# Reordering the first mixer's projections, the first loads and the last block's transposes in a two-layer trunk

## The chip, the cores and the metric

The kernel runs on one core of one Trainium2 chip. The core has five engines with a queue each: PE (TensorE, matrix products into PSUM, and PE transposes), DVE (VectorE), ACT (ScalarE), POOL (GpSimd) and SP (SyncE, which here only issues transfers). Each engine executes its queue in order. The metric is the device time of one execution in microseconds, as the median of several runs.

## The reference

A trunk of two layers works on x of 256 positions by 2048 features, all in float32. Each layer is a mixer and a squared-ReLU MLP of width 8192, each with an RMS norm ahead of it and a residual sum behind it. The mixer of the first layer has two halves that share one projection `h @ w_in`:

```
aq, ak, av, bqkv, bz, ba, bb = split(h @ w_in)
oa = diff_attention(rope(norm(aq)), rope(norm(ak)), av, lam)   # 8 heads of 128, 2 sub-heads each
bq, bk, bv = split(silu(conv4(bqkv)))
ob = gated_delta_rule(l2(bq), l2(bk), bv, g(ba), sigmoid(bb))  # 8 heads, a linear recurrence
ob = rms(ob) * silu(bz)
x = x + concat(rms(oa), ob) @ w_out
x = x + squared_relu_mlp(norm(x))
```

The second layer has a dilated attention for its mixer and the same kind of MLP.

## The kernel before

**Products.** Every large product goes through `dense` (L191). It takes 512 weight columns and the 16 chunks of 128 features that they are summed over. For each chunk ACT rounds the weights to a short float (L204, the tile `..h`) and DVE forms the remainder (L205 through the helper L107, the tile `..l`); for each of the two halves of 128 positions PE then runs three products (L210, L211, L212: high by high, high by low, low by high). So a chunk is six products of 128x128 by 128x512, and a `dense` of 16 chunks is 96 of them. Weights arrive in tiles of two chunks, loaded by `wload` (L171) on SP's queue. Four PSUM tiles (`psd`, L101) let two products be under way at once: the next one needs two tiles that the one before the last has given back.

**The activations.** `xt_block` (L261) turns 512 columns of x into four chunks: PE transposes into PSUM, ACT writes the short float with the norm's gain, DVE the remainder. PSUM for transposes has two tiles (`pst`, L102).

**What runs between the chunks.** Smaller work is written as Python generators in three streams: "g" holds the recurrences g0 to g3 (`gdn`, L600, two heads each), "s" the convolutions (`qk_conv`, `v_side`) and the attention pairs d0 to d3 (`diff`, L854), "o" the output norms. After every chunk `drip` (L182) emits the next step of one stream: "g" and "s" in turn, "o" with every fourth chunk. A stream works through its generators one behind the other. `flush` (L165) emits steps of all streams with no chunk between them, until a condition holds. A scheduler then fixes the order on each engine: earliest emitted first among what its own model of time calls ready, so a later product can be put ahead of a step whose operands are not there.

**The order of the first mixer** is written out by hand (L976 to L997): `b0 z2 bv0 b1 z0 av0 a0 b2 bv1 b3 z1 a1 av1 a2 a3`. Here `b` is queries and keys of two recurrent heads (they start a convolution and then a recurrence g), `bv` values of four recurrent heads, `z` the output gate, `a` queries and keys of an attention pair (they start d), `av` values of four attention heads. A recurrence g starts when the one before has ended and its own convolved queries and keys are there. Its steps: normalise keys (`kh`), transpose them (`kt`), products `pk` and the matrix `m`, which is written to DRAM (`scm`) and read back as small diagonal blocks (`mb`), transpose `tt1`, inversion of the blocks on DVE (`tm`, `ta`, `xc`), which goes to DRAM (`scx`) and comes back as two full matrices (`xy`, 512 KB), products `pa` with `am` and transpose `tt2`, four empty steps, two levels `lp`, `ly`, `lx`, then `lpz`, `lyz`, `pu`, `ps`, `pv`, `po`. `gdn_out` norms the result, multiplies it by the gate `sz` and transposes it (`ot`).

**The mixer's end.** Behind `a3` all recurrences are flushed, x is loaded again into `xs0` to `xs3`, and the output projection runs in two parts of eight chunks: `wo00` to `wo03` use heads 0 to 3 of each kind, then, behind another flush, `wo10` to `wo13` use the rest. The tiles `xs0`, `xs1` take the memory of the values of recurrent heads 0 to 3 and 4 to 7; `xs2`, `xs3` take that of the gate `sz`. So `xs1` can be loaded when `pu` of g3 has read its values and `xs2`, `xs3` when g3's output has been multiplied by the gate; each product is added to its `xs` tile (`add_to_x`) before its PSUM is given back.

**The beginning** (L350 to L394): eight products of a tile of zeros with itself (`pw`, L358), then the loads: the left half of the first x block (256 columns), on ACT's queue the identity and the norm's gains, then on SP the first weights of `b0`, and only then the right half of the first x block (L371). Behind the first block's transposes stand four more products into `pw` (L394), whose result nobody reads.

**Between the parts.** `next_norm` (L295) is the generator that sums the squares of a block of x (ACT) and transposes it for the next part; the last block, n = 3, does it while the next part's first product runs.

Of the kernel before, what the change touches and what calls it, by code (L numbers as in the profile page):

```python
# [19 lines left out]
P = 128  # L20
# [67 lines left out]
def trunk(  # L88
# [4 lines left out]
    nc = tc.nc  # L93
    V, S, G, E = nc.vector, nc.scalar, nc.gpsimd, nc.tensor
# [17 lines left out]
    def stt(o, a, s, b, op0, op1):  # L112
        V.scalar_tensor_tensor(out=o, in0=a, scalar=s, in1=b, op0=op0, op1=op1)
# [7 lines left out]
    def act(o, a, f, scale=1.0, bias=0.0, accum=None):  # L121
        if accum is None:
            S.activation(out=o, in_=a, func=f, scale=scale, bias=bias)  # L123
        else:
            S.activation(out=o, in_=a, func=f, scale=scale, bias=bias, accum_out=accum)
# [4 lines left out]
    def ps_t(name):  # L130
        return pst.tile([P, 512], F32, tag="t", name=name)

    def ps_m(name):
        return psm.tile([P, 512], F32, tag="m", name=name)

    def quads(t, n=4):
        return t.rearrange("p (c d) -> p c d", c=n)
# [30 lines left out]
                step(q)  # L168


    def wload(wsrc, k0, nm):  # L171
        raw = wp.tile([P, 2, 512], F32, tag="wr", name=f"{nm}r{k0}")
        off = 0
        for s in wsrc:
            m = s.shape[1]
            nc.sync.dma_start(raw[:, :, off:off + m], s[k0 * P:(k0 + 2) * P, :].rearrange("(c p) n -> p c n", p=P))
            off += m
        return raw

# [11 lines left out]
    def dense(wsrc, stat, kcs, nm, pre=(), every=1, unit=1):  # L191

        n = sum(s.shape[1] for s in wsrc)
        ps = [psd.tile([P, 512], F32, tag="d", name=f"{nm}p{h}") for h in range(NH)]
        first, last = kcs[0], kcs[-1]
        for j, kc in enumerate(kcs):
            if j % 2 == 0:
                raw = pre[j // 2] if j // 2 < len(pre) else wload(wsrc, kc, nm)
            if j % unit == 0:
                w = raw[:, j % 2:j % 2 + unit, :n]  # L200
                whs = wq[0].tile([P, unit, 512], F32R, tag="wh", name=f"{nm}h{kc}", bufs=6 // unit)[:, :, :n]
                wls = wq[0].tile([P, unit, 512], F32R, tag="wl", name=f"{nm}l{kc}", bufs=6 // unit)[:, :, :n]
                with tc.high_priority(offset=AHEAD):
                    cast[0] = S.copy(whs, w)  # L204
                    tt(wls, w, whs.bitcast(F32), ALU.subtract)  # L205
            wh, wl = whs[:, j % unit], wls[:, j % unit]
            for h in range(NH):
                sh, sl = stat(kc, h)
                o = ps[h][:, :n]
                E.matmul(o, lhsT=sh, rhs=wh, start=kc == first, stop=False)  # L210
                E.matmul(o, lhsT=sh, rhs=wl, start=False, stop=False)  # L211
                E.matmul(o, lhsT=sl, rhs=wh, start=False, stop=kc == last)  # L212
            if j % every == 0:
                drip()
        return ps
# [12 lines left out]
    def cst(name):  # L228
        lo, hi = COLS[name]
        return ca[:, lo:hi]  # L230

    ident = cst("ident")

    def transpose(o, i, k=P):
        E.transpose(o, i, ident[:k, :k])
# [12 lines left out]
    def x_tile(n, nm):  # L248
        return cp.tile([P, NH, 512], F32, tag=f"x{n}", name=f"{nm}{n}")

    def stats_block(xt, n, nm):
        for h in range(NH):
            j = sp.tile([P, 512], F32, tag="junk", name=f"{nm}j{h}")
            act(j, xt[:, h, :], AF.Square, accum=ssqp[:, h, n:n + 1])

    def stats_end(nm):
        s = sp.tile([P, NH], F32, tag="ssq2", name=nm + "s")
        rsum(s, ssqp)
        rsqrt(rstd, s, NH, 1.0 / D, nm)

    def xt_block(xt, n, norm, nm, dst, pool=None):  # L261

        if pool is not None:
            xT = pool.tile([P, 4, T], F32, tag="hT", name=nm + "T", bufs=2)
            for i in range(4):
                turn_quadrant(xt, xT, i)
                yield
        xh = xp.tile([P, 4, T], F32R, tag="xh", name=nm + "h")
        xl = xp.tile([P, 4, T], F32R, tag="xl", name=nm + "l")
        dst.append((xh, xl))  # L270
        for c2 in range(2):
            if pool is None:
                t = quads(ps_t(f"{nm}t{c2}"), 2)
                for c in range(2):
                    for h in range(NH):
                        k = c2 * 2 + c
                        transpose(t[:, c, h * P:(h + 1) * P], xt[:, h, k * P:(k + 1) * P])
            else:
                t = xT[:, 2 * c2:2 * c2 + 2, :]
            for c in range(2):  # L280
                k = c2 * 2 + c
                g = gt[:, norm * 16 + n * 4 + k:norm * 16 + n * 4 + k + 1]
                act(xh[:, k, :], t[:, c, :], AF.Identity, scale=g)
                stt(xl[:, k, :], t[:, c, :], g, xh[:, k, :].bitcast(F32), ALU.mult, ALU.subtract)
            yield

    def turn_quadrant(src, dst, i):

        q = slice(32 * i, 32 * i + 32)
        sv = src[q].rearrange("p h (c j f) -> p h c j f", c=4, j=4)  # L290
        for j in range(4):
            dv = dst[32 * j:32 * j + 32].rearrange("p c (h t) -> p h c t", h=NH)
            V.transpose(out=dv[:, :, :, q], in_=sv[:, :, :, j, :])  # L293

    def next_norm(n, norm, nm, dst, pool=None):  # L295

        stats_block(xs[n], n, nm + "s")
        yield from xt_block(xs[n], n, norm, nm, dst, pool if n < 3 else None)
        if n == 3:
            stats_end(nm + "e")  # L300
            yield
# [41 lines left out]
    xv = x[0].rearrange("(h p) d -> p h d", p=P)  # L343
# [3 lines left out]
    def b_cols(s):  # L347
        return [win[:, 3072 + s * 256:3328 + s * 256], win[:, 4096 + s * 256:4352 + s * 256]]
# [6 lines left out]
    pw = ps_m("pw")  # L355
# [3 lines left out]
    xq = [x_tile(n, "xq") for n in range(4)]  # L359
    pre = []  # L360
    for n in range(4):
        if n == 0:
            nc.sync.dma_start(xq[0][:, :, :256], xv[:, :, :256])
            nc.scalar.dma_start(ca[:, :P], consts[:, :P])
            nc.scalar.dma_start(grow0, ab_norm[0].rearrange("(c p) -> c p", p=P))
        else:
            nc.sync.dma_start(xq[n], xv[:, :, n * 512:(n + 1) * 512])
        if n < 3:
            pre.append(wload(b_cols(0), 2 * n, "b0"))
        if n == 0:  # L370
            nc.sync.dma_start(xq[0][:, :, 256:], xv[:, :, 256:512])  # L371
    with ExitStack() as mix:
        wq[0] = mix.enter_context(tc.tile_pool(name="wq0", bufs=1))
        op = mix.enter_context(tc.tile_pool(name="op", bufs=1))
# [13 lines left out]
        for n in range(4):  # L388
            for _ in xt_block(xq[n], n, 0, f"xa{n}", xb):
                pass  # L390
            if n == 0:

                for _ in range(4):
                    E.matmul(pw[:, :P], lhsT=ident, rhs=xq[0][:, 1, 256:384], start=True, stop=True)  # L394


        cga = cp.tile([P, NH, 2, 64], F32, name="cga")
# [538 lines left out]
        def do_b(s, pre=()):  # L936
            ps = dense(b_cols(s), xstat, KC16, f"b{s}", pre)
            flush(lambda: "rstd" in ready)
            streams["s"].append(qk_conv(raw_evac(ps, f"b{s}raw"), f"b{s}raw", s, qks))
            streams["g"].append(gdn_of(s))  # L940
# [6 lines left out]
        def do_bv(g):  # L947
            ps = dense([win[:, 5120 + g * 512:5632 + g * 512]], xstat, KC16, f"bv{g}")
            rv = raw_evac(ps, f"bv{g}raw")
            vbs[g] = cp.tile([P, NH, 4, P], F32, tag=f"x{g}", name=f"vb{g}")  # L950
            streams["s"].append(v_side(rv, f"bv{g}raw", g, vbs[g], f"bv{g}"))

        def do_a(s):
            ps = dense([win[:, s * 256:(s + 1) * 256], win[:, 1024 + s * 256:1280 + s * 256]], xstat, KC16, f"a{s}")
            r = raw_evac(ps, f"a{s}raw")
            streams["s"].append(diff_of(r, s))
# [6 lines left out]
        def do_av(g):  # L963
            ps = dense([win[:, 2048 + g * 512:2560 + g * 512]], xstat, KC16, f"av{g}")
            va = mp.tile([P, NH, 512], F32, tag="va", name=f"va{g}", bufs=2)
            for h in range(NH):
                act(va[:, h, :], ps[h], AF.Identity, scale=rstd[:, h:h + 1])
            vas[g] = va
# [11 lines left out]
        bz_evac(ps, 776, 248, "z2")  # L980
        streams["s"].append(gates(ga, gb))
        do_bv(0)
        do_b(1)
        ps = dense([win[:, 6144:6656]], xstat, KC16, "z0")
        bz_evac(ps, 0, 512, "z0")
        ready.add("z0")
        do_av(0)
        do_a(0)
        do_b(2)
        do_bv(1)  # L990
        do_b(3)
        ps = dense([win[:, 6656:6920]], xstat, KC16, "z1", every=2)
        bz_evac(ps, 512, 264, "z1")
        ready.add("z1")
        do_a(1)
        do_av(1)
        do_a(2)  # L997
        do_a(3)
# [185 lines left out]
```

## Time and profile before

| what | us |
|---|---|
| median of 3 runs | 2296.64 (2295.28 to 2297.88) |
| the profiled execution's own time | 2296.41 |
| its span, first instruction to last | 2294.6 |
| PE busy in the span | 2281.6 |

The first mixer fills the span up to about 514 us. `L210 PE MATMUL wo13p` means that PE ran a product of line 210 into the PSUM tile of the product `wo13`; digits that are only buffer numbers are left out of names, so `xs` stands for all four blocks. A product of the steady stream is shown with about 0.39 us, but they overlap: one starts every 0.23 us. Times are counted from the span's start.

### The profile page before, as it was taken

To read this page: it belongs to the slowest core of one execution; us is meant where nothing else is said; L and a number is where in the kernel's file an instruction comes from. 1 tells how busy PE (TensorE), PEld (TensorE's weight loads), DVE (VectorE), ACT (ScalarE), POOL (GpSimd) and SP (SyncE) were. 2 spreads that over 40 slices of the span, in tenths; PEclk is the share of its full clock that TensorE was granted. 3 is DMA by queue.
4 is the path that set the end of the run, shared out by engine and by line. 5 is a ranking of instruction groups with operands and counts; after the bars stand their busy time and mean duration, and the time that the engine had idled before them with its cause. 6 is when DMAs were issued, how large, how long until landed. Compare 5 with 4: busy or idle time off the path is not lost.

```text
span 2294.6 us, 29903 instructions
## 1 busy us (share of the span) xinstructions
PE 2281.6 (99%) x10544; PEld 1890.9 (82%) x10544; DVE 1666.3 (73%) x3027; ACT 1195.8 (52%) x1865; POOL 5.7 (0%) x15
## 2 busy tenths in 40 slices
PE   9999999999999999999999999999999999999999
PEld 8887878788888888888888888888888888888887
DVE  6868787867747846846888888986775775775774
ACT  7657656655534534534545555555543543543553
POOL 0000000000000000000000000000000000000000
PEclk9999999999999999999999999999999999999999
DMA  8655455456666666666666555555666666666665
GB/s 257 185 171 167 138 176 144 140 174 195 200 193 190 196 194 189 196 197 190 192 190 199 177 180 176 174 184 165 193 193 195 193 194 195 192 196 193 188 208 165
DMA packets 271482, 426.54 MB, mean 186 GB/s; under 512 B 22322, under 2 KB 102372, under 8 KB 271332
## 3 DMA queue, kind: packets, MB, share of 16 engines
q1 hardware_dynamic: 271156, 424.56, 61.1%
q8 instruction: 82, 1.34, 0.2%
q14 instruction: 68, 0.56, 0.1%
q10 hardware_dynamic: 176, 0.07, 0.0%
HBM read 420.11 MB, written 4.46 MB: 185 GB/s over the span
## 4 chain that ended last, share of the span: by engine, by line
PE 95%; DVE 3%; DMA 1%; ACT 1%; issue 0%; SPq 0%; ACTq 0%
PE m_0p L211 3%; PE n_2p L211 3%; PE n_1p L212 3%; PE n_0p L212 3%; PE m_3p L212 3%; PE m_3p L210 3%; PE m_2p L212 3%; PE m_2p L210 3%; PE m_1p L212 3%; PE m_1p L210 3%; PE n_1p L211 3%; PE n_0p L210 3%; PE n_2p L212 3%; PE m_0p L212 3%; PE n_2p L210 3%; PE n_0p L211 3%
## 5 line engine op out<-in xcount | busy, mean ns | idle before, releaser
L107 DVE TENSOR_TENSOR n_3l<-n_3r,n_3h 128x1024 fp32r<-128x1024 f32 x64 | 78.4, 1224 | 76.8 <-ACT n_3h L204 76.7
L107 DVE TENSOR_TENSOR n_2l<-n_2r,n_2h 128x1024 fp32r<-128x1024 f32 x64 | 78.4, 1224 | 76.8 <-ACT n_2h L204 76.7
L107 DVE TENSOR_TENSOR m_0l<-m_0r,m_0h 128x1024 fp32r<-128x1024 f32 x64 | 78.1, 1225 | 73.4 <-ACT m_0h L204 73.0
L107 DVE TENSOR_TENSOR n_1l<-n_1r,n_1h 128x1024 fp32r<-128x1024 f32 x64 | 78.4, 1224 | 67.8 <-ACT n_1h L204 67.2
L204 ACT CAST n_2h<-n_2r 128x1024 fp32r<-128x1024 f32 x64 | 67.5, 1054 | 100.2 <-PE n_2p L212 59.9
L204 ACT CAST n_3h<-n_3r 128x1024 fp32r<-128x1024 f32 x64 | 67.5, 1054 | 100.2 <-PE n_3p L212 59.9
L204 ACT CAST m_0h<-m_0r 128x1024 fp32r<-128x1024 f32 x64 | 67.1, 1054 | 97.2 <-PE m_0p L212 59.9
L204 ACT CAST n_1h<-n_1r 128x1024 fp32r<-128x1024 f32 x64 | 67.5, 1054 | 92.8 <-PE n_1p L212 59.9
L107 DVE TENSOR_TENSOR m_1l<-m_1r,m_1h 128x1024 fp32r<-128x1024 f32 x64 | 78.4, 1225 | 36.9 <-ACT m_1h L204 35.9
L204 ACT CAST m_1h<-m_1r 128x1024 fp32r<-128x1024 f32 x64 | 67.5, 1054 | 66.6 <-PE m_1p L212 38.3
L204 ACT CAST m_3h<-m_3r 128x1024 fp32r<-128x1024 f32 x64 | 67.5, 1054 | 57.3 <-PE m_3p L212 39.9
L204 ACT CAST n_0h<-n_0r 128x1024 fp32r<-128x1024 f32 x64 | 67.5, 1054 | 57.3 <-PE n_0p L212 39.9
L204 ACT CAST m_2h<-m_2r 128x1024 fp32r<-128x1024 f32 x64 | 67.5, 1054 | 57.3 <-PE m_2p L212 39.9
L107 DVE TENSOR_TENSOR m_3l<-m_3r,m_3h 128x1024 fp32r<-128x1024 f32 x64 | 78.4, 1225 | 25.8 <-ACT m_3h L204 24.0
L107 DVE TENSOR_TENSOR n_0l<-n_0r,n_0h 128x1024 fp32r<-128x1024 f32 x64 | 78.4, 1225 | 25.8 <-ACT n_0h L204 24.0
L107 DVE TENSOR_TENSOR m_2l<-m_2r,m_2h 128x1024 fp32r<-128x1024 f32 x64 | 78.4, 1225 | 25.7 <-ACT m_2h L204 24.0
L293 DVE STREAM_TRANSPOSE m_0hT<-m_0r 32x256 f32<-32x256 f32 x128 | 55.8, 436 | 5.8 <-ACT m_0r L123 3.7
L293 DVE STREAM_TRANSPOSE m_2hT<-m_2r 32x256 f32<-32x256 f32 x128 | 55.8, 436 | 5.7 <-ACT m_2r L123 3.6
L293 DVE STREAM_TRANSPOSE m_1hT<-m_1r 32x256 f32<-32x256 f32 x128 | 55.8, 436 | 5.7 <-ACT m_1r L123 3.6
L293 DVE STREAM_TRANSPOSE m_3hT<-m_3r 32x256 f32<-32x256 f32 x128 | 55.8, 436 | 5.7 <-ACT m_3r L123 3.6
L210 PE MATMUL n_0p<-n_0h,m_0hh 128*128 128x512 f32 x64 | 24.9, 389 | 0.0
L211 PE MATMUL n_0p<-n_0l,m_0hh 128*128 128x512 f32 x64 | 24.9, 389 | 0.0
(2555 smaller groups left out, 7396.9 us busy)
## 6 DMA issues: line engine op xcount, KB each, us to landing
m_0r<-in_mlp_w_dram SPq DMA_DIRECT2D x64, 512.0 KB, 4.2
m_1r<-in_mlp_w_dram SPq DMA_DIRECT2D x64, 512.0 KB, 4.0
m_2r<-in_mlp_w_dram SPq DMA_DIRECT2D x64, 512.0 KB, 4.3
m_3r<-in_mlp_w_dram SPq DMA_DIRECT2D x64, 512.0 KB, 4.2
n_0r<-in_mlp_w_dram SPq DMA_DIRECT2D x64, 512.0 KB, 4.1
n_1r<-in_mlp_w_dram SPq DMA_DIRECT2D x64, 512.0 KB, 4.2
n_2r<-in_mlp_w_dram SPq DMA_DIRECT2D x64, 512.0 KB, 4.4
n_3r<-in_mlp_w_dram SPq DMA_DIRECT2D x64, 512.0 KB, 4.2
```

The lines of the kernel that those rows point to most:

```text
L107: V.tensor_tensor(out=o, in0=a, in1=b, op=op)
L204: cast[0] = S.copy(whs, w)
L210: E.matmul(o, lhsT=sh, rhs=wh, start=kc == first, stop=False)
L211: E.matmul(o, lhsT=sh, rhs=wl, start=False, stop=False)
L212: E.matmul(o, lhsT=sl, rhs=wh, start=False, stop=kc == last)
L293: V.transpose(out=dv[:, :, :, q], in_=sv[:, :, :, j, :])
```

## The change

There are four edits.

1. In the first mixer's list `av0` and `a0` move from behind `z0` to a place ahead of `b1`, and `a1` moves from behind `z1` to a place ahead of `bv1`. The new order is `b0 z2 bv0 av0 a0 b1 z0 b2 a1 bv1 b3 z1 av1 a2 a3`.
2. The first weights of `b0` are loaded through ACT's queue, and the right half of the first x block is issued on SP right behind its left half.
3. The four extra products into `pw` are left out.
4. For the last block, `next_norm` gives its turn away once between the sums of squares and the transposes, so that the transposes are emitted one turn of the stream "s" (two chunks) later. This holds for the three places where the next part begins: the first MLP, the second mixer and the second MLP.

```diff
-    def wload(wsrc, k0, nm):
+    def wload(wsrc, k0, nm, queue=nc.sync):
...
-            nc.sync.dma_start(raw[:, :, off:off + m], s[k0 * P:(k0 + 2) * P, :].rearrange("(c p) n -> p c n", p=P))
+            queue.dma_start(raw[:, :, off:off + m], s[k0 * P:(k0 + 2) * P, :].rearrange("(c p) n -> p c n", p=P))
...
         stats_block(xs[n], n, nm + "s")
+        if n == 3:
+            yield
         yield from xt_block(xs[n], n, norm, nm, dst, pool if n < 3 else None)
...
             nc.scalar.dma_start(grow0, ab_norm[0].rearrange("(c p) -> c p", p=P))
+            nc.sync.dma_start(xq[0][:, :, 256:], xv[:, :, 256:512])
...
-            pre.append(wload(b_cols(0), 2 * n, "b0"))
-        if n == 0:
-            nc.sync.dma_start(xq[0][:, :, 256:], xv[:, :, 256:512])
+            pre.append(wload(b_cols(0), 2 * n, "b0", nc.scalar if n == 0 else nc.sync))
...
-            if n == 0:
-
-                for _ in range(4):
-                    E.matmul(pw[:, :P], lhsT=ident, rhs=xq[0][:, 1, 256:384], start=True, stop=True)
...
         do_bv(0)
+        do_av(0)
+        do_a(0)
         do_b(1)
...
-        do_av(0)
-        do_a(0)
         do_b(2)
+        do_a(1)
         do_bv(1)
...
-        do_a(1)
         do_av(1)
```

## The prediction

> **What bounds the kernel now.** I read the page first, then the waits of PE, then stretches and the timeline where a wait stands. The page:
>
> ```profile
> span 2294.6 us, 29903 instructions
> ...
> PE 2281.6 (99%) x10544; PEld 1890.9 (82%) x10544; DVE 1666.3 (73%) x3027; ACT 1195.8 (52%) x1865; POOL 5.7 (0%) x15
> ```
>
> PE is idle for 2294.6 - 2281.6 = 13.0 us of the span, and the change neither adds nor removes a product, but for the four into `pw`. So all that an order can win is idle time, time at a low clock and those four. The view of waits, for PE over the whole run (us in total, times, longest):
>
> ```profile
> PE g2lp L721 <- DMA g2xy<-scx: 2.6, 1, 2.6
> ...
> PE g0tt L235 <- DVE g0am L107: 1.4, 1, 1.4
> PE xa0t L235 <- DMA xq<-in_x_dram: 0.8, 1, 0.8
> PE d0s L900 <- DVE g1am L107: 0.6, 1, 0.6
> ```
>
> Three of the four belong to the recurrences: g2 waits for the inverted blocks to come back from DRAM, g0 and (through d0's slot in the queue) g1 wait for DVE. The longest wait costs more than itself. Two stretches, ahead of it and behind it (busy of PE, PEld, DVE, ACT, POOL, then the granted clock, DMA share, GB/s):
>
> ```profile
> 308.00:318.60 10.60, 10.60 (x47) 8.46 (x46) 10.60 (x25) 5.74 (x10) 0.00 (x0) 1.00 0.62 174
> ...
> 321.70:325.10 3.40, 3.40 (x14) 2.92 (x13) 2.17 (x5) 0.62 (x1) 0.00 (x0) 0.50 0.62 201
> ```
>
> Ahead of the wait DVE is busy for 10.60 of 10.60 us: the inversion shares it with everything else and is late. Behind the wait the clock is 0.50 for 3.40 us, in which 1.7 us of work are lost. So the waits of the recurrences cost 2.6 + 1.7 + 1.4 + 0.6 = 6.3 us. This is what edit 1 can win.
>
> **The start (edits 2 and 3).** The timeline of the first microseconds (start, length, engine, what):
>
> ```profile
> 1.22 0.99 SPq L176 DMA_DIRECT2D b0r<-in_ab_w_in_dram  x2
> ...
> 1.67 1.28 ACT L123 ACT_TABLE_LOAD   x1 [1.67 <-PEq L1170]
> 2.25 0.47 SPq L371 DMA_DIRECT2D xq<-in_x_dram  x1
> ...
> 5.37 1.11 PE L235 MATMUL xa0t<-ca,xq 128*128 128x128 f32 x4
> ...
> 5.79 0.62 ACT L204 CAST b0h<-b0r 128x512 fp32r<-128x512 f32 x1 [2.61 <-DMA b0r<-in_ab_w_in_dram]
> ...
> 6.53 0.47 ACT L123 ACTIVATE xa0h<-xa0t,gt 128x256 fp32r<-128x256 f32 x1
> ...
> 7.05 0.48 DVE L113 SCALAR_TENSOR_TENSOR xa0l<-xa0t,gt,xa0h 128x256 fp32r<-128x256 f32 x1
> ...
> 7.33 1.09 PE L235 MATMUL xa0t<-ca,xq 128*128 128x128 f32 x4 [0.84 <-DMA xq<-in_x_dram]
> ...
> 8.21 1.92 PE L394 MATMUL pw<-xq,ca 128*128 128x128 f32 x8
> ...
> 9.78 0.77 PE L210 MATMUL b0p<-b0h,xa0h 128*128 128x512 f32 x1
> ...
> 10.35 0.63 PE L211 MATMUL b0p<-b0l,xa0h 128*128 128x512 f32 x1
> 10.78 0.54 PE L212 MATMUL b0p<-b0h,xa0l 128*128 128x512 f32 x1
> ...
> 12.06 0.39 PE L212 MATMUL b0p<-b0h,xa0l 128*128 128x512 f32 x1
> ...
> 12.29 0.40 PE L210 MATMUL b0p<-b0h,xa0h 128*128 128x512 f32 x1
> ```
>
> The right half of x is issued at 2.25 and used at 7.33, 5.1 us later. Moved ahead of the two weight issues it goes out 0.99 us earlier, at about 1.2, and can be used at about 6.3, before PE ends the left half's transposes (5.37 + 1.11 = 6.48). So the wait of 0.84 goes, and the second four transposes end at about 7.6. The first product of `b0` needs the short float of the first chunk of x (6.53 + 0.47 = 7.0) and of the weights (5.79 + 0.62 = 6.4); the third needs the remainder (7.05 + 0.48 = 7.5). With `pw` gone, it can start at about 7.6 instead of 9.78: **-2.2 us**. Nothing else hid the `pw` products: the first product stood behind them with its operands ready.
>
> What edit 2 adds: the first weights go out on ACT behind its two issues. Two issues cost 0.99 us by the row at 1.22, so they leave at about 1.7 to 2.6 instead of 1.2 to 2.2, and the ACT table load moves from 1.67 to about 2.7; it hides in the 2.61 us in which ACT waits for the weights anyway. The weights come some 0.4 us later, at 6.2, still ahead of 7.6. If the scheduler puts the table load between the issues instead, they leave 1.28 us later still, the remainder of the weights comes at about 9, and -1.1 of the 2.2 is left. Bytes do not change, and the transfers are at their peak for the whole stretch, so the blocks behind come when they came, or up to 1 us sooner. Bounds of the term: -3.9 to 0.
>
> The upper gain has to do with the clock. The first products start 0.43 us apart (10.35 to 10.78), those from 12.06 on 0.23 us apart: PE runs at half speed until about 11 us. The Trainium skill's page "TensorE: Matmul & The Clock Gate", section "Part 1: The HAM clock gate (the "warmup" mystery)", says that the array begins at half its clock and is let go after a window of about 3.4 us of sustained work, the windows running freely. By that rule the four `pw` products were there to fill such a window: without them, should PE idle in their place, full speed comes a window later, and the start would gain 0.5 us only; if the real products fill it, nothing is lost. From the rows alone: in place of the idle 0.84 and of `pw` there is real work at once, so the speed-up comes at 11 us or one slow stretch (3.40 us, 1.7 us of work) earlier or later. I take neither.
>
> **Edit 1 before the end.** I counted the turns of the three streams along both lists. In the old list d0 starts behind g1's convolution; in the new one g1's convolution stands behind d0 in the stream "s", so g1 waits four of its turns when g0 is done. Each recurrence has nine turns, 18 chunks, from `pk` to `lp`, in both orders, and DVE must share these with others: in the old order g0 with a convolution (waited 1.4), g1 with d0 (0.6; d0's own products gave PE something to do), g2 with a convolution and d1 (2.6, 1.7 of clock). In the new order g0 shares with no convolution, g1 with that of `b2` and no attention, g2 with that of `b3`. So g0 should wait less, g1 takes the place that g2 had, and g2 looks like the old g0. I forecast 0.9 + 4.3 + 1.4 = 6.6 in place of 6.3, and call it **0**. Bounds: all three gone, -6.3; all three like the old g2 (4.3 each), +6.6.
>
> **Edit 1 at the mixer's end.** Here the four lost turns come due. By the count `pk` of g3 moves from chunk 8 of `a3` to the flush behind `a3`. Rows of g3 and of what waits for it, from the tiles, from SP's timeline and from the chain:
>
> ```profile
> L651 PE MATMUL g3pk<-g3khT x8: 272/275/275, 384.4 to 385.2; 128*128 128x128 f32 x8
> ...
> 389.42 0.37 SPq L657 DMA_DIRECT2D scm<-g3m  x1
> ...
> 391.60 0.33 SPq L659 DMA_DIRECT2D g3mb<-scm  x1
> ...
> 404.36 0.90 SPq L700 DMA_DIRECT2D scx<-g3xc  x2
> 406.74 0.38 SPq L703 DMA_DIRECT2D g3xy<-scx  x1
> ...
> 411.78 0.89 PE g3lp L721 x8
> ...
> 454.87 0.33 PE g3ot L235
> ...
> 455.10 0.89 SPq L1007 DMA_DIRECT2D xs<-in_x_dram  x2
> ...
> L107 DVE TENSOR_TENSOR xs<-wo02p,xs x2: 685/688/692, 460.9 to 462.1; 128x512 f32<-128x512 f32 x2
> ...
> L210 PE MATMUL wo00p<-wo00h,g0oh x4: 390/438/586, 399.9 to 402.9; 128*128 128x512 f32 x4
> ...
> L210 PE MATMUL wo10p<-wo10h,g2oh x4: 389/389/389, 467.0 to 469.0; 128*128 128x512 f32 x4
> ...
> 399.00:467.00 68.00, 67.49 (x361) 53.31 (x360) 56.07 (x169) 43.74 (x117) 0.95 (x1) 1.00 0.49 153
> ```
>
> Let T be the start of `wo00`, 399.9. PE has work from T to `wo10`, 67.1 us (busy 67.49 of 68), plus about 1.4 for `pk` and `tt1`, which move in. Now `wo10` needs the PSUM of `wo02`, hence `xs2`, hence g3's gated output: from `ot` (454.9) to the end of the second sum (462.1 + 0.7 = 462.8) are 7.9 us. Today that ends 4.2 us ahead of `wo10`. New: `pk` at T instead of 15.5 us ahead of it. From `pk` to `lp` it took 411.8 - 384.4 = 27.4 at the chunks' pace; in a flush the least is products 0.9, `m` 1.4, write to read 2.2, read to write of the inversion 404.36 - 391.60 = 12.8, to the next read 2.4, to `lp` 5.0: 24.7. From `lp` to `ot` it took 43.1, with d3 on the same DVE and PSUM; d3 keeps its place, so more of the new stretch is free of it: 36 to 43. So `wo10` may start at T + 24.7 + 36 + 7.9 = T + 68.6 up to T + 27.4 + 43.1 + 7.9 = T + 78.4, and PE has work until T + 68.5: **0 to +10 us**. DVE, busy 56.07 of 68, has room for the 5 or 6 us that move in, but not at every moment. I take **+2**, near the low end: the scheduler may put later products ahead of any step that is not ready, and d3's own work ends some 20 us ahead of g3's.
>
> **Edit 4.** The boundary to the first MLP, timeline of PE:
>
> ```profile
> 513.74 0.44 PE L235 MATMUL xb3t<-ca,xs 128*128 128x128 f32 x2
> 514.42 0.55 PE L235 MATMUL xb3t<-ca,xs 128*128 128x128 f32 x3 [0.24 <-DVE xs L107]
> 514.82 0.74 PE L210 MATMUL m_0p<-m_0h,xb0h 128*128 128x512 f32 x2
> 515.39 0.49 PE L235 MATMUL xb3t<-ca,xs 128*128 128x128 f32 x3
> 516.08 0.50 PE L211 MATMUL m_0p<-m_0l,xb0h 128*128 128x512 f32 x1 [0.19 <-DVE m_0l L107]
> ```
>
> PE already fills the gap before the new weights are rounded with these eight transposes, though they are emitted behind the first six products. Emitted later, they are still the only thing that is ready, so I expect them in the same place: **0**. If they do leave the gap, it stays empty for their 8 x 0.11 = 0.9 us, three times: +2.6; if only the waits for the last sums go (0.24 and the like), -0.5.
>
> **Sum.** -2.2 + 0 + 2 + 0 = -0.2, on the profiled execution's 2296.41 (1.8 around the span, 0.2 below the median of the runs shown): 2296.2, and 2296.4 beside the median. A difference under 0.2%, 4.6 us, is about what a measurement of this kernel cannot tell from none.
>
> **Rivals.** (a) *Nothing takes the place of g2's wait.* The convolutions need less of DVE than d1 did, g1 waits about a microsecond, and the end just fits: -2.2 - 4.3 + 0 = -6.5, 2290. For it: in the new order no inversion shares DVE with an attention pair, and 308 to 318.6 was full because of one. Against: nine turns were too short for g0 as well, without one. (b) *The recurrences' tail sets the mixer's end*: slower. If `ot` of g3 comes later than T + 60.6, each microsecond more is idle PE between `wo03` and `wo10`; at T + 70.5 it is 10, with a slow stretch behind it 11.7, so -2.2 + 11.7 = +9.5, 2306; in its middle 2302. For it: the head start lost, 15.5 us, is far more than the 4.2 us of slack. Against: the other products that can be put ahead. (c) *The change does little of what it says*: the table load comes between the issues, the clock rises a stretch later, the transposes and the end are where they were: -1.1 + 1.7 = +0.6, 2297. (d) *By the clock page's rule* with PE idle in place of `pw`: the start gains 2.2 - 1.7 = 0.5, the rest as in the sum: 2298.
>
> **Chances.** The sum as worked out 0.38, (c) and (d) 0.06 each, together 0.50 within 0.2%; (a) 0.28; (b) 0.22. The range goes from (a) at 2290 to the middle of (b), with the clock, at 2303; without (a) and (b) it would be 2292 to 2301.
>
> **What would show it.** The first product of `b0` at about 7.6, or after 9 (c). In PE's waits `g1lp` or `g1tt` in the place of `g2lp`; if no recurrence waits over 1 us, (a). A gap of PE ahead of `wo10` or `wo03`, released by DVE's `xs` or by the transfer of `xs`, with g3's `pk` at T or later: (b). The transposes `xb3t`, `xc3t`, `xd3t` in the gap or behind it. I am wrong if the order on PE differs so much that chunks, not waits, changed their pace, or if a wait appears in the second mixer, which the change leaves alone.

## The result, and the profile after

| | before | after |
|---|---|---|
| median of 15 runs, us | 2295.99 (2292.12 to 2299.44) | 2300.32 (2298.10 to 2302.43) |
| ratio of the medians | | 1.0019, 95% interval 1.0012 to 1.0026 |
| profiled execution, us | 2296.41 | 2301.3 |

The change makes the kernel 4.3 us slower. The forecast was 2296.4, 0.2 us less than the median of before known then (2296.64). First the head of the page after (the span, then busy time, share and instructions of each engine):

```profile
span 2299.5 us, 29877 instructions
...
PE 2281.6 (99%) x10536; PEld 1892.4 (82%) x10536; DVE 1672.3 (73%) x3027; ACT 1196.0 (52%) x1865; POOL 5.6 (0%) x15
```

PE is busy for the same 2281.6 us, though eight records fewer stand there (the four products left out, each recorded as two passes). So the 4.9 us of span are idle time of PE by this count, 2299.5 - 2281.6 = 17.9 in place of 13.0; a lower clock hides in the busy time, since it stretches products. Where the idle time lies, by the view of PE's waits (us in total, times, longest):

```profile
PE g2tt L235 <- DVE g2am L107: 3.0, 1, 3.0
PE xa1t L235 <- DMA xq<-in_x_dram: 2.6, 1, 2.6
PE g0ly L724 <- DVE g0P L107: 1.9, 1, 1.9
...
PE b0p L210 <- ACT b0h L204: 1.1, 1, 1.1
PE d2ot L235 <- DVE d2o L117: 1.0, 1, 1.0
PE g3lp L718 <- DMA g3xy<-scx: 1.0, 1, 1.0
```

Two of these, 2.6 and 1.1, are at the start, and both are new; the old wait of 0.8 for the right half of x has gone. The timeline of the first microseconds after (start, length, engine, what, idle time before it):

```profile
1.23 0.47 SPq L368 DMA_DIRECT2D xq<-in_x_dram  x1
...
1.67 1.28 ACT L123 ACT_TABLE_LOAD   x1 [1.67 <-PEq L1167]
1.73 1.05 ACTq L176 DMA_DIRECT2D b0r<-in_ab_w_in_dram  x2
1.75 0.46 SPq L370 DMA_DIRECT2D xq<-in_x_dram  x1
2.25 1.27 SPq L176 DMA_DIRECT2D b0r<-in_ab_w_in_dram  x2
...
5.38 1.39 PE L235 MATMUL xa0t<-ca,xq 128*128 128x128 f32 x8
...
9.41 1.06 PE L235 MATMUL xa1t<-ca,xq 128*128 128x128 f32 x4 [2.64 <-DMA xq<-in_x_dram]
...
10.89 1.14 ACT L204 CAST b0h<-b0r 128x512 fp32r<-128x512 f32 x2 [3.02 <-DMA b0r<-in_ab_w_in_dram]
...
11.56 1.22 PE L210 MATMUL b0p<-b0h,xa0h 128*128 128x512 f32 x2 [1.09 <-ACT b0h L204]
```

The right half of x does what was forecast: issued at 1.23, and all eight transposes run in one piece from 5.38, without the old wait of 0.84. But the weights, issued at 1.73 to 2.78 as forecast, are rounded at 10.89, not at 6.2, and the first product runs at 11.56, not at 7.6. The transfers of the first 30 us, by issue (how many, KB each, median us from issue to landing), after:

```profile
b0r<-in_ab_w_in_dram SPq DMA_DIRECT2D x14, 256.0 KB, 4.3
...
b0r<-in_ab_w_in_dram ACTq DMA_DIRECT2D x2, 256.0 KB, 8.6
```

and before, where all sixteen go through SP's queue:

```profile
b0r<-in_ab_w_in_dram SPq DMA_DIRECT2D x16, 256.0 KB, 5.4
```

The 4.3 and the 5.4 are not to be set beside the 8.6: they are medians over 30 us, and most of these transfers were issued after the first rush. The issues from 2.7 to 3.2 us alone give, for the next weights on SP's queue in the same execution:

```profile
b0r<-in_ab_w_in_dram SPq DMA_DIRECT2D x2, 256.0 KB, 8.2
```

The second x block (512 KB, issued on SP at 1.75) took 7.5. So SP's transfers of these microseconds are nearly as slow as ACT's. What the weights lost is their place: before, they stood near the head of SP's queue, and their last part took 4.0 us. An estimate from these rows: while ACT's queue brought its 512 KB (there at about 10.9), SP's brought the 512 KB of x (9.3) and the 512 KB of weights behind it (about 11), about twice as much. PE has nothing to do meanwhile, and the clock follows. Stretches after (length, busy of PE, PEld, DVE, ACT, POOL, granted clock, DMA share, GB/s):

```profile
6.10:9.40 3.30, 0.67 (x6) 0.45 (x5) 1.41 (x3) 1.39 (x3) 0.00 (x0) 1.00 1.02 366
...
9.50:16.20 6.70, 5.61 (x17) 4.29 (x18) 3.28 (x6) 3.73 (x9) 0.00 (x0) 0.50 1.03 364
...
136.70:138.70 2.00, 0.05 (x1) 0.05 (x1) 2.00 (x6) 0.62 (x1) 0.00 (x0) 1.00 0.53 125
139.20:142.60 3.40, 3.40 (x12) 2.87 (x11) 2.81 (x6) 0.00 (x0) 0.00 (x0) 0.50 0.40 109
327.30:330.30 3.00, 0.07 (x1) 0.00 (x0) 3.00 (x7) 0.00 (x0) 0.00 (x0) 1.00 0.85 180
330.30:333.70 3.40, 3.33 (x10) 2.88 (x11) 2.99 (x6) 1.10 (x2) 0.00 (x0) 0.50 0.80 225
...
399.60:471.80 72.20, 69.79 (x377) 55.44 (x375) 60.29 (x185) 46.16 (x121) 0.95 (x1) 1.00 0.48 148
```

The DMA engines are full (share 1.02): the late weights are no lack of bytes moved, only of these bytes. PE is busy 0.67 of 3.30 us, and for the 6.7 us behind that the clock is 0.50. The next two pairs of rows are the waits of g0 and g2, each with PE empty and DVE full, and the 3.40 us at 0.50 behind each: g2 had such a pair before as well, g0 had not. The last row is the flush with `wo00` to `wo03`, taken up below.

A boundary that is easy to read is the first product of `z2`, the end of `b0`. From the tiles, before and after (min/median/max ns, first and last start):

```profile
L210 PE MATMUL z2p<-z2h,xa0h x8: 280/283/285, 35.1 to 37.6; 128*128 128x264 f32 x8
```

```profile
L210 PE MATMUL z2p<-z2h,xa0h x8: 280/283/285, 38.0 to 40.5; 128*128 128x264 f32 x8
```

So 2.9 of the 4.9 us are lost by the end of `b0`. From there to the first product of `wo10` it is 471.8 - 38.0 = 433.8 after, 467.0 - 35.1 = 431.9 before: 1.9 more. PE's idle time ahead of the flush is the same (361.60 - 356.52 = 5.1 after, 363.90 - 358.86 = 5.0 before); in the flush it is 2.4 in place of 0.5, which is the 1.9. From `wo10` to the end of the span it is 1827.7 against 1827.6: nothing.

### The profile page after: what moved, and what is told of

The parts are those of the page before. It is cut to its first block, busy times and chain, and to the rows that moved or that the text cites. A ratio compares the mean times of both kernels' runs of the same rounds, so it can differ in the third digit from the quotient of the medians.

```text
span 2299.5 us, 29877 instructions
## 1 busy us (share of the span) xinstructions
PE 2281.6 (99%) x10536; PEld 1892.4 (82%) x10536; DVE 1672.3 (73%) x3027; ACT 1196.0 (52%) x1865; POOL 5.6 (0%) x15
## 4 chain that ended last, share of the span: by engine, by line
PE 93%; DVE 4%; DMA 1%; ACT 1%; issue 0%; ACTq 0%; SPq 0%; DVEq 0%
PE m_0p L211 3%; PE m_0p L212 3%; PE n_2p L212 3%; PE n_2p L211 3%; PE n_1p L212 3%; PE n_0p L212 3%; PE m_3p L210 3%; PE m_2p L211 3%; PE m_2p L210 3%; PE m_1p L211 3%; PE n_0p L210 3%; PE n_1p L211 3%; PE m_1p L212 3%; PE m_3p L212 3%; PE m_3p L211 3%; PE m_1p L210 3%
```

## The experiments

Two theories stood against each other for the loss at the start, and one question for the rest. **Queue:** the weights are late because they go through ACT's queue. **Products:** the four `pw` products had kept PE busy and its clock up, and without them the start is slow. For the rest: does the new order (edit 1) cost anything by itself? Thirteen more runs were made. "Start" below is the first product of `z2` in that kernel's profile; the ratio is to the kernel before on the same chip, with its 95% interval. Each ratio's resolution is some 0.09%, 2 us.

| kernel | what it is | ratio | start |
|---|---|---|---|
| before | | 1 | 35.1 |
| e1_start | edits 2 and 3 | 1.0010 (1.0001 to 1.0019) | 36.5 |
| e2_order | edit 1 | 1.0003 (0.9994 to 1.0012) | 33.9 |
| e3_turn | edit 4 | 0.9999 (0.9990 to 1.0008) | 33.5 |
| e4_nopw | edit 3 | 0.9990 (0.9981 to 0.9999) | 32.5 |
| e5_spx | edit 3, right half of x early, weights on SP | 0.9993 (0.9984 to 1.0001) | 33.5 |
| e11_sponly | all but the weights' queue | 0.9999 (0.9990 to 1.0007) | 33.3 |
| e12_after | the changed kernel again | 1.0018 (1.0009 to 1.0026) | 37.0 |
| e14_actw | weights on ACT, `pw` kept | 1.0005 (0.9996 to 1.0014) | 34.6 |
| e17_pwback | changed kernel, `pw` put back | 1.0008 (0.9999 to 1.0017) | 37.7 |
| e6_actx | edit 3, right half of x on ACT, weights on SP | 0.9999 (0.9990 to 1.0007) | 33.5 |
| e9_late | before, g1 four turns later | 0.9988 (0.9979 to 0.9997) | 33.1 |
| e15_best4 | edit 3, g1 four turns later | 0.9986 (0.9977 to 0.9995) | 34.6 |
| e16_best2 | edit 3, g1 two turns later | 0.9988 (0.9980 to 0.9997) | 32.7 |

The start varies between executions of the same code: the four kernels that leave it alone (before, e2, e3, e9) show 35.1, 33.9, 33.5 and 33.1, a mean of 33.9. Before's profiled execution is the latest of them. The three with both edits 2 and 3 (after, e1, e12) show 38.0, 36.5 and 37.0, a mean of 37.2: 3.3 later. A profile is one execution: e12's took 2296.63, well under the median of its runs, 2299.83, and e9's 2290.20, the least of its runs.

### Each part by itself

e1_start, edits 2 and 3 of the diff above, alone:

> Edits 2 and 3 alone (first weights through ACT's queue, right half of x earlier on SP, no pw products behind the first block), the projections in the old order. Theory L (the loads lose it): the first weights share the engines with SP's queue and land about 10.4 us after the start, PE waits 2.6 us for the second x block and 1.1 us for the weights, two slow stretches of the clock follow, b0 ends near 38.2 instead of 35.2: +3.0 us, about 2299. Theory O (the new order of the projections loses it all, and the late start would be caught up behind b0): 2296, no change.

Measured: +0.10%, 2298.42 beside 2295.89, and a first product at 10.2. The start alone is slower by about 2.5 us (the interval reaches from 0.2 to 4.4), where -2.2 had been forecast; the two waits of the changed kernel are there (`xa1t` 1.9, `b0p` 1.1).

e2_order, edit 1 alone:

> Edit 1 alone, the old start. Theory L: b0 ends at 35.2; g2's transpose waits about 3 us for DVE and g0's ly about 2, each with a slow stretch of the clock, and PE is idle for about 2 us in the flush: +1.8 us in all, about 2298. Theory O: the whole difference, +4.3 us, about 2300. If the waits move with the phase of the start, they are of another size and the sum lies anywhere from 0 to +4.

Measured: +0.03%, not to be told from nothing. Its waits of PE, beside those that the prediction shows of before:

```profile
PE g2tt L235 <- DVE g2am L107: 3.5, 1, 3.5
...
PE d2ot L235 <- DVE d2o L117: 1.1, 1, 1.1
```

g2 still waits longest, 3.5 us ahead of `tt2` in place of 2.6 ahead of `lp`; g0 waits 0.4, and g1 not at all. The wait moved up inside the same recurrence.

e3_turn, edit 4 alone:

> Edit 4 alone, the extra turn before the last block's transposes. Theory of the prediction: the eight transposes stay in the gap before the first rounded weights, PE waits 0.1 + 0.24 + 0.19 us there as before, at all three places: 0 us, 2296. Rival: they leave the gap, +0.9 us at each place, +2.6 us, 2298.6.

Measured: -0.01%. The three boundaries are as they were. Timeline of PE after, at the first of them:

```profile
518.60 0.44 PE L235 MATMUL xb3t<-ca,xs 128*128 128x128 f32 x2
519.28 0.55 PE L235 MATMUL xb3t<-ca,xs 128*128 128x128 f32 x3 [0.24 <-DVE xs L107]
519.67 0.73 PE L210 MATMUL m_0p<-m_0h,xb0h 128*128 128x512 f32 x2
520.24 0.49 PE L235 MATMUL xb3t<-ca,xs 128*128 128x128 f32 x3
520.93 0.50 PE L211 MATMUL m_0p<-m_0l,xb0h 128*128 128x512 f32 x1 [0.20 <-DVE m_0l L107]
```

Row for row it is the old sequence, in the same gap, with the same wait of 0.24: what is emitted a turn later is run at the same place, since nothing else is ready.

e4_nopw, edit 3 alone:

> Edit 3 alone: the four products into pw are left out, all loads as before. Theory L: the second transposes still wait 0.84 us for the right half of x, the first product of b0 starts at about 8.5 instead of 9.78, b0 ends 1.3 us sooner: about 2294.7. Rival C (the clock rule): PE idles somewhere in that place, full speed comes a stretch of 3.4 us later, which takes 1.7 us back: b0 ends 0.4 us later or no sooner, 2296 to 2297.

Measured: -0.10%, and a first product of `b0` at 7.74, right behind the transposes: 9.78 - 7.74 = 2.0 us sooner, and 2.4 in the medians. Before's 9.78 is a late one, though: with the same start e2, e3 and e9 have 9.09, 8.71 and 8.23, so against the mean of the four, 8.95, it is 1.2. With the weights on SP, leaving `pw` out is no loss, and by this ratio a small gain. So the products can't be the cause by themselves.

### The queue

e5_spx keeps SP for the weights but moves the right half of x ahead of them:

```diff
             nc.scalar.dma_start(grow0, ab_norm[0].rearrange("(c p) -> c p", p=P))
+            nc.sync.dma_start(xq[0][:, :, 256:], xv[:, :, 256:512])
...
-        if n == 0:
-            nc.sync.dma_start(xq[0][:, :, 256:], xv[:, :, 256:512])
```

with `pw` left out too.

> Edit 3, and of edit 2 the half that stays on SP: no pw products behind the first block, the right half of the first x block issued right behind its left half, the first weights of b0 behind it on SP (not on ACT). Old order of the projections. Theory A (ACT's queue is what loses the start): no wait for the second x block, the first product of b0 near 7.7 to 8.2, b0 ends near 32.5 to 33; 2293, as without pw alone or up to 0.8 us better. Rival (the weights come too late wherever they are queued behind x): a wait of about 1 us for the weights and slow stretches as with both queues, 2297.

Measured: -0.07%, first product at 8.4, behind a wait of 1.1 for the rounded weights. ACT rounds them at 7.75, behind two pieces of x, and the first product stands 0.7 us later than in e4. The time is the one of theory A, 2293.02; that nothing would wait was wrong.

e11_sponly is the changed kernel with one thing undone, the queue:

```diff
-            pre.append(wload(b_cols(0), 2 * n, "b0", nc.scalar if n == 0 else nc.sync))
+            pre.append(wload(b_cols(0), 2 * n, "b0"))
```

> The changed kernel with one thing undone: the first weights of b0 go through SP's queue again. Theory A: the start is the one of the kernel without pw, 4 to 5 us sooner at the end of b0 than the changed kernel, and the new order costs nothing against the old: 2293 to 2296. Rival (the new order and the late start lose together): still above 2298.

and e12_after, on the same chip, is the changed kernel again:

> The changed kernel itself again, unchanged, beside the others on one chip. If the parts add up (start +2.5, order 0, turn 0): 2298 to 2299. If late start and new order lose together: 2300, and g0's ly waits near 2 us again with a slow stretch of the clock behind it.

Measured: 0.9999 and 1.0018. The queue of two transfers of 256 KB takes away all that the change loses, 2299.83 - 2294.60 = 5.2 us; the first product is at 8.1 in e11 and at 10.4 in e12. This is the one pair that decides. The first weights of e11, by the issues from 1.7 to 2.75 us:

```profile
b0r<-in_ab_w_in_dram SPq DMA_DIRECT2D x2, 256.0 KB, 4.1
```

In e12, issued on ACT's queue in the same microsecond, they took 7.4, and the next weights on SP's queue 6.2. ACT rounds them at 7.40 in e11 and at 9.76 in e12. Whether the parts add up in e12 or lose together stays open: its time is that of the second forecast, but g0's wait of 1.7 there has no slow stretch behind it.

e14_actw does the reverse, the queue alone, with `pw` kept (the edit of `wload` and its call above, nothing else):

> The kernel before with one thing changed: the first weights of b0 go through ACT's queue (SP then issues the right half of x earlier by itself). The four pw products stay. Theory A (the late weights alone make the start late): weights land 7 to 8.6 us after their issue, the first product of b0 starts at 10 to 11, b0 ends near 36 to 37, 2298. Rival C (leaving out pw is half of it): pw fills the place ahead of the second x block, the clock doesn't fall, b0 ends near 35, 2296.

Measured: +0.05%, between -0.04% and +0.14%, 2296.65, and `b0` ends at 34.6: nearer to rival C than to theory A. Stretches of e14:

```profile
6.10:9.40 3.30, 2.50 (x18) 2.10 (x16) 1.41 (x3) 1.57 (x4) 0.00 (x0) 1.00 1.07 378
...
9.50:16.20 6.70, 6.32 (x30) 4.63 (x31) 6.17 (x12) 6.45 (x17) 0.00 (x0) 1.00 1.08 388
```

Here PE is busy for 2.50 of the 3.30 us in which it was busy for 0.67 after the change, and the clock stays at 1.00 behind it. The weights are late here as well (rounded at 9.21), but what is left of the gap, 1.3 us of waits, costs only itself.

e17_pwback puts `pw` back into the changed kernel (and the line of the right half back to its old place; on SP it still follows the left half):

> The changed kernel with one thing undone: the four pw products are there again (weights on ACT's queue, new order, extra turn as changed). Theory P (the pair loses it): pw fills the place ahead of the second x block, the clock doesn't fall for two stretches, b0 ends near 34.7 to 35.5, about 2.5 us sooner than in the changed kernel: 2296 to 2297. Rival W (late weights and new order lose together, whatever stands in the gap): b0 ends near 37, 2299 to 2300.

Measured: +0.08%, about half of the loss, with an interval that reaches from nothing to nearly all of it. The median, 2297.22, is near theory P's; `b0` ends at 37.7, as rival W had it. Its profiled execution is not the clean case that e14 was:

```profile
6.10:9.40 3.30, 2.12 (x18) 1.72 (x16) 1.41 (x3) 1.38 (x3) 0.00 (x0) 1.00 1.07 380
9.50:12.80 3.30, 1.23 (x4) 0.76 (x5) 1.25 (x3) 1.90 (x4) 0.00 (x0) 0.99 1.07 393
12.90:16.20 3.30, 3.30 (x11) 2.66 (x10) 2.35 (x6) 2.19 (x7) 0.00 (x0) 0.51 0.95 329
```

The products fill the first stretch, but the weights came at 10.90, so the gap stands in the second one (1.23 of 3.30) and the slow clock in the third. Up to here e14 and e17 issue the same transfers, and the landing differs by 1.7 us: filler covers a late transfer only if the transfer is not later than the filler.

e6_actx puts another 256 KB on ACT's queue, the right half of x, and leaves the weights on SP:

```diff
+            nc.scalar.dma_start(xq[0][:, :, 256:], xv[:, :, 256:512])
...
-            nc.sync.dma_start(xq[0][:, :, 256:], xv[:, :, 256:512])
```

with `pw` left out.

> No pw products, the first weights on SP, and the right half of the first x block (256 KB) on ACT's queue instead of SP's. Theory Q (a transfer on the second queue comes late beside a full first one, whatever it carries): it lands 5 to 7 us after its issue, the second transposes wait for it 1 to 2 us, b0 ends at 34 to 35, 2295 to 2296. Rival S (only the 512 KB of the weights were too much for that queue): no wait, as with both on SP, 2293.

Measured: -0.01%, 2294.26, and `b0` ends at 33.5. Its timeline:

```profile
1.79 0.42 ACTq L366 DMA_DIRECT2D xq<-in_x_dram  x1
...
8.55 0.63 PE L235 MATMUL xa0t<-ca,xq 128*128 128x128 f32 x4 [2.05 <-DMA xq<-in_x_dram]
```

Issued 0.46 us earlier than on SP before (2.25), the half is used 1.2 us later (8.55 against 7.33); in the six other kernels that load it on SP behind the first weights (e2, e3, e4, e9, e15, e16) it is used between 6.96 and 7.87. So the delay is not the weights' own: a transfer on ACT's queue beside SP's full one came later here too. Against e4, which gained 0.10%, this placing costs about 0.09%, no more than the two ratios leave uncertain.

### The order, and a version that is faster than both

e9_late takes the lost turns by themselves: g1 starts four turns later, in the old order.

```diff
         def gdn_of(s):
+            if s == 1:
+                for _ in range(4):
+                    yield
```

> The kernel before, but g1 begins four of its turns later (four empty turns are put ahead of it); nothing else is moved. Theory of the prediction's tail: g3's first products fall into the flush behind a3 as in the new order, PE is idle there for about 2 us (ahead of d2's transpose and of g3's lp): 2296 + 2 = 2298. Rival (the flush takes the lost turns for nothing, the idle time there comes from the order of the projections): no idle time over 0.5 us in the flush, 2296.

Measured: -0.12%, faster, not slower. Its waits:

```profile
PE g3lp L721 <- DMA g3xy<-scx: 1.2, 1, 1.2
PE d2ot L235 <- DVE d2o L117: 1.0, 1, 1.0
PE d1t L235 <- DVE d1qk L107: 0.6, 1, 0.6
PE g0tt L235 <- DVE g0am L107: 0.5, 1, 0.5
PE g2tt L235 <- DVE g2am L107: 0.5, 1, 0.5
```

and the stretch from the end of `a3` to `wo10`, then the one that was slow in before:

```profile
388.60:460.80 72.20, 69.64 (x376) 55.42 (x375) 60.24 (x185) 46.13 (x121) 0.95 (x1) 1.00 0.46 148
...
321.70:325.10 3.40, 3.40 (x15) 2.49 (x14) 2.63 (x10) 2.61 (x8) 0.00 (x0) 1.00 0.91 299
```

The flush is as long as in the changed kernel, 72.20 us with 2.6 idle; but g2's wait has gone (0.5 in place of 2.6), and with it the slow stretch. What the later start costs in the flush is more than made up in the middle. Why g2 no longer waits there was not tried. The prediction's reason, that the inversion is late because `d1` shares DVE with it, does not explain it: by the tiles, `d1qk` is formed from 306 to 320 in e9, partly beside g2's inversion (303 to 316), and from 318 to 328 before, behind it (303 to 314). The inversion even ends later in e9; but `lp` is run 9.7 us behind its end there (326.0) and 7.6 before (321.2).

e15_best4 and e16_best2 join this, with four and with two turns, to edit 3:

> The kernel before without the four pw products, and g1 four of its turns later. If the two gains add up (-2.4 and -3.4): 2289.5. If the wait of g2 comes back with the start's shift: 2293.

> The same with g1 two turns later instead of four. Theory: each turn moves g2's inversion away from d1's work on DVE and g3's first products towards the flush; with two turns g2 still waits 1 to 2 us and the flush is idle about 1 us: between 2290 and 2293. If the gain has to do with d1 alone, two turns are not enough and g2 waits 2.5 us: 2293.

Measured: 0.9986 and 0.9988, 2291.94 and 2292.35 beside 2294.78. Both are faster than both kernels. Whether the two gains add up can't be told (-0.10% and -0.12% apart, -0.14% together, each with some 0.09% to either side), nor can they be told from e4 or e9. g2 waits 0.5 and 0.9.

## Why the prediction was right or wrong

**The start was the failing step.** The term was -2.2; by e1 it is +2.5 in the medians, by the starts +3.3. Its parts, in order. "It goes out 0.99 us earlier, at about 1.2": right, 1.23. The wait of 0.84 goes: right. "They leave at about 1.7 to 2.6": right, 1.73 to 2.78, and the table load took nothing from them, so the reason that rival (c) gave did not occur. "With `pw` gone, it can start at about 7.6": right for PE, as e4's 7.74 shows, though 9.78 was the latest of four starts, so that -2.2 was too much in any case (e4: 1.2 under their mean). What failed is **"The weights come some 0.4 us later, at 6.2, still ahead of 7.6"**. It added the later issue to a landing time that the weights had near the head of SP's queue, 4.0 us before and 4.1 in e11. On ACT's queue they took 8.6, 7.2, 7.4, 6.9 and 8.6 us (after, e1, e12, e14, e17), and the next weights on SP's, issued about a microsecond later in the same kernels, took 8.2, 6.2, 6.2, 5.7 and 7.9. So the weights came among the transfers that had stood behind them. The sentence "the transfers are at their peak for the whole stretch, so the blocks behind come when they came" was half of the answer: with the engines full, a transfer that loses its place in front must be later, and I did not ask which one that is. The bounds, -3.9 to 0, had no case on the other side.

The Trainium skill, page "DMA: Bandwidth & Descriptors", section "Issuing engines are not separate DMA queues", says that transfers from any engine run on the same 16 DMA engines and interleave, and that issuing from several engines saves only the issue time. The trace agrees: 0.99 us of issue moved off SP, and the weights landed with SP's transfers of the same microseconds (8.6 beside 8.2 us), no longer ahead of them (4.1 in e11).

**The clock.** "If the real products fill it, nothing is lost" and "I take neither" was the second weak place. With the weights at 6.2 it would mostly have held: e4, e5, e11 and e16 have no slow stretch at the start in their profiles. e15 has one: with the first loads of e4, PE waited 1.98 us there for the right half of x, and ran at half clock behind it:

```profile
8.30:11.70 3.40, 3.40 (x11) 2.62 (x10) 1.61 (x4) 1.31 (x3) 0.00 (x0) 0.50 1.05 368
```

After a wait of 2.05 in e6 there is none. With the weights at 10.9 PE was busy for 0.67 of 3.30 us and ran 6.7 us at half clock. The losses add: the first product stands 2 to 4 us later than with SP's weights (10.2 to 11.6 against 7.7 to 8.4), and then comes work at half clock, 1.7 us for each such stretch that is full of products. That the gap sets the clock is the reading of e14 beside after; that leaving out `pw` gains 0.10% with the weights on SP and costs 0.05 to 0.10% with them on ACT (e1 less e14, e12 less e17) fits it, but neither of these two differences is larger than its uncertainty.

The Trainium skill, page "TensorE: Matmul & The Clock Gate", section "Part 1: The HAM clock gate (the "warmup" mystery)", says that an idle window of about 3.4 us, in windows that run freely, brings the half clock back. The trace agrees only in part: the half clock came, but behind a gap of 2.64 us, shorter than that, with 0.67 us of work in the 3.30. So rival (d), PE idle in place of `pw` and half clock behind it, had part of the mechanism and missed the size, since it had the weights in time.

**Edit 1 before the end**: the sum, 0, fits what e2 shows, but by luck, since its parts are others. Waits and clock were to go from 6.3 to 6.6; e2 has 3.5 + 0.4 of waits and one slow stretch of 1.7, together 5.6. "g1 takes the place that g2 had, and g2 looks like the old g0" was wrong: g1 did not wait in after, e2, e11 or e12 (1.6 in e17), and g2 kept the longest wait of the recurrences (3.0, 3.5, 4.4, 2.9, and 3.1 in e17). Rival (a), that nothing would take the place of g2's wait, is out for the same reason. e9 reached it by another way.

**Edit 1 at the mixer's end**: +2, and the flush after has 72.20 - 69.79 = 2.4 us idle where before had 68.00 - 67.49 = 0.5 by the prediction's row: +1.9, at full clock. The tiles of after:

```profile
L210 PE MATMUL wo00p<-wo00h,g0oh x4: 397/480/580, 401.8 to 407.5; 128*128 128x512 f32 x4
...
L648 PE MATMUL g3pk<-g3khT x8: 275/275/377, 400.1 to 401.0; 128*128 128x128 f32 x8
...
L718 PE MATMUL g3lp<-g3xy,g3mT x16: 273/275/377, 427.1 to 436.7; 128*128 128x128 f32 x16
...
L235 PE MATMUL g3ot<-ca,g3o x4: 272/328/328, 462.2 to 463.0; 128*128 128x128 f32 x4
...
L107 DVE TENSOR_TENSOR xs<-wo02p,xs x2: 680/685/690, 467.5 to 468.1; 128x512 f32<-128x512 f32 x2
...
L210 PE MATMUL wo10p<-wo10h,g2oh x4: 389/389/389, 471.8 to 473.9; 128*128 128x512 f32 x4
```

T, the start of `wo00`, is 401.8, and `pk` stands 1.7 us ahead of it, in the flush as counted and no longer 15.5 ahead; 27.0 to `lp` (24.7 to 27.4 forecast), 35.1 to `ot` (36 to 43), 6.6 to the end of `xs2` at 468.8 (7.9). That is 3.0 us ahead of `wo10`, so rival (b) did not occur: `wo10` waits for no `xs`. The size was right, the place was not, and that the size fits is luck: the idle time is inside the flush, 1.0 ahead of g3's `lp` and 1.0 ahead of `d2ot`. The same two waits stand in the other profiles of the new order (e2, e11, e12, e17: 0.9 to 1.2 each) and in e9.

**Edit 4**: 0, right.

**Do the parts add up?** +0.10% (e1) + 0.03% (e2) - 0.01% (e3) = +0.12%, against 0.18 to 0.19% for the whole. The intervals allow it. Edits 1 and 4 on top of each start (e12 less e1, e11 less e5, e17 less e14, and e2 + e3) come to +0.08, +0.06, +0.03 and +0.02%: all above zero, none by more than its uncertainty, so the order may cost about a microsecond, and this stays open. The 1.9 us that after's profile loses between `z2` and `wo10` is the idle time of the flush, which every profile of the new order shows. Busy time up to there is the same as before, 426.3 us, though one slow stretch more (1.7) is in it; what offsets that was not found. That 2300.32 lies near the 2302 of rival (b) is chance: (b)'s wait did not occur.

## What to carry to other kernels

Don't take a transfer's landing time from the head of one queue to another queue: while the first queue keeps the DMA engines full, what is needed first belongs at its head, and not on a second queue to save an issue. Don't set a median over a long stretch beside a transfer of the first rush. Before filler products are removed, ask what PE does if the next operands are late: if the answer is nothing, the gap may cost half-clock time behind it as well. And a later start of a side chain can be faster (e9, for a reason not found here): try its turn count as well.

## What the hardware showed that was not expected

**Landing time goes by the place in the queue.** 256 KB of weights took 4.0 to 4.1 us from issue to landing near the head of SP's queue (before, e11), 6.9 to 8.6 on ACT's queue beside it (five kernels), and 5.7 to 8.2 on SP's behind 512 KB of x in the same kernels, with the engines at a share of 1.02 (after). How the engines divide themselves between two queues was not measured by itself.

**Whether a wait costs clock is partly chance.** g0's wait of 1.9 us in after was followed by a slow stretch (139.2 to 142.6 at 0.50), g2's waits of 2.9 us in e12 and in e5 and of 3.1 in e17 by none. A reading of one profile can be off by 1.7 us for each such wait.

**The beginning is not repeatable.** With the same first loads, `b0` ended at 35.1 us in one profile (before) and at 33.1 in another (e9). `pw`'s last products took 1.92 us for eight records in before, at 8.21, and 1.06 in e9, at 7.42: by this pace PE was still at half speed in before and at full speed in e9. The view's clock reads 1.00 in both, so the pace alone tells it. A change of 2 us in the first 15 us can't be judged from one profile on each side.
